# Low halves of the weights made by GpSimd instead of VectorE in the attention stages and, for every second chunk, in the opening

## The chip, the cores and the metric

The kernel runs on one core of a Trainium2 chip. The metric is the device time of one execution in microseconds, lower is better. All matrix products are done by TensorE; VectorE (DVE), ScalarE (ACT) and GpSimd (POOL) do elementwise work on data in SBUF, VectorE and ScalarE also on PSUM; SyncE (SP) issues most of the loads from device memory.

## The reference, cut to what matters

Two transformer blocks in float32 over 512 tokens of width 1024: a first block of two layers, and a second block with a recurrent branch, chunked attention, cross-attention to a memory of 256 rows, and a mixture of experts. The parts that this change touches are the products with the attention weights:

```python
for layer in range(DEPTH):                       # DEPTH = 2
    mod = sc @ w_mod[layer] + b_mod[layer]       # six vectors of 1024
    h = rmsnorm(x, g_attn[layer]) * (1.0 + scale1) + shift1
    proj = h @ w_in                              # q, k, v of three kinds of attention, 16 heads of 64 in all
    ...                                          # differential, dilated and forgetting attention
    x = x + gate1 * (o @ w_out)
    ...                                          # convolution, gated feed-forward part
# second block
...                                              # recurrent branch and chunk_band_attention: q, k, v from h @ w_in
k = (mem_n @ wk).reshape(b, m, N_XHEADS, XHEAD_DIM)   # keys and values of the memory
v = (mem_n @ wv).reshape(b, m, N_XHEADS, XHEAD_DIM)
...                                              # cross-attention, router, experts
```

## The kernel before, in words

Precision. Every float32 operand of a large product is split in two: a high half, which is the value rounded to the type that TensorE multiplies fast (`fp32r`), and a low half, the value minus the high half. A product is three matrix multiplications: high by high, high by low, low by high (`mm3`, L189). Weights are split on the chip. `wchunk` (L169) does this for one chunk of, mostly, 128 x 1024 values: SP loads it into a raw buffer `wr`, ScalarE copies it into `wh` (L176), VectorE subtracts (`wl` = `wr` - `wh`, L177). `wr`, `wh` and `wl` have three buffers each (for some chunks, asked for with `x=True`, `wh` and `wl` come from a second pool of three). So the load of a chunk can't be issued before the subtraction three chunks earlier has read its raw buffer, and `wh` and `wl` wait for TensorE's last use three chunks earlier.

Stages. The opening (`memory_kv`, L599) computes the keys and values of the memory for the much later cross-attention: 8 chunks of `xk_w` by `linear_fm`, 8 of `xv_w` by `linear_tm` (two per group of 256 columns), and, ahead of the last group, the 2 chunks of the first group of `w_qkv`. Between them it loads `x`, and computes parts of `mod` on VectorE: `mod_part` (L376) loads a 128 x 1024 piece of `w_mod` and multiplies and sums it with one instruction (L384). Results go to device memory by DMAs that GpSimd issues (`kd` L624, `vd` L636).

Then each layer of the first block runs `attention` (L829). Groups of 256 columns of `w_qkv`, two chunks each, are computed by `tm_pieces` (L474): one first group of values, ten more groups. While a group's second tile of tokens is computed, the first chunk of the next group is split (L502); after the fourth tile the second chunk, with a higher priority (L505). The matrix products are woven with the heads: scores (L396), row minimum (L399, VectorE) and exponential (L401, ScalarE), scaling (L422 or L427, VectorE), transposes (L444), a split of the transposed probabilities (L186, L187), the product with the values (L457), `operands` (L513), which turns queries and keys and splits them into `op` tiles, and `ends`, which starts the product with `w_out` (3 chunks). In layer 0 VectorE also does 27 of the `mod` parts here. GpSimd fills the unused half of an `op` tile with zeros (L554) or copies `op` tiles (L842, L843). `chunk_attention` (L1222) of the second block is built the same way: six groups, 12 chunks. The feed-forward parts, `w_out2`, the cross-attention and the experts are outside the change.

Order. Each engine works through its own queue in order. The order is planned when the program is built, by priorities and by which instructions are then expected to be ready, and `high_priority` moves instructions ahead; in the attentions the order of TensorE is the written one (`manual_schedule`).

Of the kernel before, what the change touches and what calls it, by code (L numbers as in the profile page):

```python
# [124 lines left out]
class Block:  # L125
# [43 lines left out]
    def wchunk(self, src, n, x=False):  # L169
        nc = self.nc  # L170
        raw = self.wp.tile([P, WCH], F32, tag="wr", name="wr", bufs=3)[:, :n]
        pool, nb = (self.wx, 3) if x else (self.wp, 3)
        hi = pool.tile([P, WCH], F32R, tag="wh", name="wh", bufs=nb)[:, :n]
        lo = pool.tile([P, WCH], F32R, tag="wl", name="wl", bufs=nb)[:, :n]
        nc.sync.dma_start(out=raw, in_=src)
        nc.scalar.copy(hi, raw)  # L176
        nc.vector.tensor_sub(lo, raw, hi)  # L177
        return hi, lo

    def split(self, src, hi, lo, hi_eng=None):  # L180

        nc = self.nc
        if hi_eng is nc.vector:
            nc.vector.tensor_copy(hi, src)
        else:
            nc.scalar.copy(hi, src)  # L186
        return nc.vector.tensor_sub(lo, src, hi)  # L187
# [406 lines left out]
def first_block(B, debug=None):  # L594
    with B.pool("const1") as c1:
        return first_block_(B, c1, debug)


def memory_kv(B, pool, load_x, mods, early, nxt):  # L599

    nc, I = B.nc, B.I
    kd, vd = B.kd, B.vd
    gm = pool.tile([P, KD], F32, name="gm")
    nc.sync.dma_start(out=gm, in_=I["mem_g"])
    mt = [pool.tile([P, 256], F32, name=f"m{k}") for k in range(KD)]
    nm = Norm(B, KD, D, n=256, pool=pool)
    for k in range(KD):
        nc.sync.dma_start(out=mt[k], in_=I["memT"][k])
        nm.add(k, mt[k], HALF[0])
    mn = []  # L610
    for k in range(KD):
        mn.append((pool.tile([P, 256], F32R, name=f"mh{k}"), pool.tile([P, 256], F32R, name=f"ml{k}")))
        B.gsplit(mt[k], gm[:, k:k + 1], mn[k])
    r = pool.tile([P, 2], F32, name="rm")
    nc.vector.tensor_copy(r, nm.rstd())
    R = B.spread_to(r, pool.tile([P, 256], F32, name="Rm"))

    def buf():
        return pool.tile([P, 256], F32, tag="kv", name="kv", bufs=4)

    for n in range(KD):
        t = buf()
        nc.vector.tensor_mul(t, B.linear_fm(I["xk_w"][n], mn, KD, n=256)[:, :256], R)
        nc.gpsimd.dma_start(out=kd[n], in_=t)  # L624
        load_x(XA[n])
        mods(MA[n])
    for c in range(4):
        mods(MA[8 + c])
        if c == 1:
            early()  # L630
        if c == 3:
            got = nxt()
        for j, ps in enumerate(B.linear_tm(I["xv_w"][c], mn, ntt=2)):
            t = buf()
            nc.scalar.mul(t, ps, r[:, j:j + 1])
            nc.gpsimd.dma_start(out=vd[j, :, c * 256:(c + 1) * 256], in_=t)  # L636
    return got


def first_block_(B, const, debug):  # L640
    tc, nc, I = B.tc, B.nc, B.I
# [38 lines left out]
    def load_x(n):  # L680
        for k in xs[:n]:
            nc.sync.dma_start(out=B.x[k], in_=I["xT"][k])
            nm.add(k, B.x[k], slice(0, T))
        del xs[:n]

    got = None
    if debug is None:
        got = memory_kv(B, pool, load_x, some, nm.early, lambda: B.wtm(I["w_qkv"][0, 0], x=True))
    else:
        load_x(KD)  # L690
# [11 lines left out]
    for layer in range(2):  # L702
# [31 lines left out]
        def late(n):  # L734
            B.mod_part(layer, mod, bm, todo[:n])
            del todo[:n]

        with B.pool("op") as op:
            o = [op.tile([P, T], F32, name=f"o{k}") for k in range(KD)]
            with B.pool("at") as at:  # L740
                B.at, B.nop = at, 14
                begun, oh = attention(B, layer, h, first, o, lam, sg, fb, late, I["w_out"][layer])
            if debug is not None and layer == debug[1] and debug[0] == "o":
                for k in range(KD):
                    nc.sync.dma_start(out=I["dbg"][k], in_=o[k])
                return
            B.acc_set(True)
            wb = ExitStack()
            wb.enter_context(B.extra())

            up = I["w_up"][layer]
            nm = Norm(B, KD, D)
            got = B.residual([I["w_out"][layer, n] for n in range(KD)], oh, KD, mod[:, 16:24], [nm], 2,
                             lambda: [B.wtile(up[j], KD, x=True) for j in (KF, 0, KF + 1)], begun=begun)
# [259 lines left out]
def second_block_dense(B, first, h3, debug=None):  # L1014

    tc, nc, I = B.tc, B.nc, B.I
    nm, h = mixer2(B, first)
    if debug == "m":
        return dump(B)
# [66 lines left out]
def mixer2(B, first):  # L1086


    tc, nc, I = B.tc, B.nc, B.I
# [27 lines left out]
    with B.pool("ym") as ym:  # L1117
# [76 lines left out]
                B.lnexp()  # L1194
        B.acc_set(False)
        st = {}
        with B.pool("at2") as at:
            B.at, B.nop = at, 9
            chunk_attention(B, at, h, r12, gn, ya, nr, Rr, st)
        na = st["na"]  # L1200

        def part(n, a, y, R):
            ps = B.acc()
            B.fm(ps, B.wtile(I["w_out2"][n][:, a * T:(a + 1) * T], 4), y)
            t = B.tt("yo")
            nc.vector.tensor_mul(t, ps, R)
            nc.vector.tensor_add(B.x[n], B.x[n], t)
# [705 lines left out]
```

## Time and profile before

| | |
|---|---|
| median of 3 runs | 2441.1 us (2438.98 to 2444.31) |
| the profiled execution | 2438.89 us, span 2437.1 us, mean granted TensorE clock 0.98 |
| TensorE busy | 2284.5 us (94% of the span) |
| VectorE busy | 1768.8 us (73%) |
| ScalarE busy | 1402.7 us (58%) |
| GpSimd busy | 142.9 us (6%), 136 instructions |
| L177, VectorE, all chunks | 284 instructions, 317.2 us |
| chain that ended last | TensorE 71%, VectorE 11%, L177 alone 2% |

How to read it: the span runs from the first to the last instruction of the profiled execution. Busy times of engines overlap. The chain is followed back from the last instruction, at each step to what released it, or to the instruction before it on its engine; its shares say where time was spent with nothing else late. [...] In the line groups, "x" is a count, then come the busy time in us, the mean of one in ns, the idle time of the engine just ahead of them and what ended it. A name like `wl<-wr,wh` is output and inputs.

### The profile page before, as it was taken

What the parts mean: (1) busy time and instruction counts of PE and PEld (TensorE: products, weight loads), DVE (VectorE), ACT (ScalarE), POOL (GpSimd) and SP (SyncE); (2) the same over time, 40 slices, a digit from 0 to 9 for tenths busy, and PEclk for the clock granted to TensorE, in tenths of its full rate; (3) what the DMA queues carried; (4) which work ended last, traced back from release to release, by engine and by line L of the source; (5) the groups of instructions that cost most, each with busy time, mean ns of one, the idle gap of its engine ahead of it and who ended that gap; (6) DMA issues with size and microseconds to landing.
All of it is one profiled execution on the core that took longest, in us unless ns stands there. A gap on an engine that the chain in (4) does not pass through costs nothing.

```text
span 2437.1 us, 33968 instructions
## 1 busy us (share of the span) xinstructions
PE 2284.5 (94%) x12341; PEld 1877.2 (77%) x12341; DVE 1768.8 (73%) x3246; ACT 1402.7 (58%) x2279; POOL 142.9 (6%) x136
## 2 busy tenths in 40 slices
PE   6888989999999899899999998999979999999998
PEld 6878968888888789788888887978756666666665
DVE  7899878745756897664434467687658888888888
ACT  4576764322333867643223446655427888888886
POOL 0000000000000000000000000100011111111110
PEclk9999999999999999999999999999979999999999
DMA  9623415635643111032233232214379999999992
GB/s 325 190 87 105 140 60 170 202 115 180 195 143 93 44 62 55 33 104 95 80 111 95 80 98 79 61 57 151 110 270 325 362 364 358 357 354 353 353 348 93
DMA packets 131872, 417.83 MB, mean 171 GB/s; under 512 B 22937, under 2 KB 30105, under 8 KB 131696
## 3 DMA queue, kind: packets, MB, share of 16 engines
q1 hardware_dynamic: 122832, 401.03, 48.2%
q0 software_dynamic: 8864, 14.54, 2.2%
q8 instruction: 99, 1.62, 0.3%
q14 instruction: 77, 0.63, 0.1%
HBM read 411.46 MB, written 20.19 MB: 177 GB/s over the span
## 4 chain that ended last, share of the span: by engine, by line
PE 71%; DVE 11%; issue 8%; ACT 6%; DMA 3%; SPq 0%; POOL 0%; DVEq 0%; ACTq 0%; POOLq 0%
PE acc L191 12%; PE acc L192 12%; PE acc L193 12%; PE acc L1512 8%; PE acc L1530 7%; PE acc L1513 7%; PE acc L490 2%; PE acc L491 2%; PE acc L492 2%; DVE wl L177 2%; PE s L396 1%; PE pv L457 1%; PE pt L444 1%; DVE wm L384 1%; ACT wh L176 1%
## 5 line engine op out<-in xcount | busy, mean ns | idle before, releaser
L176 ACT CAST wh<-wr 128x1024 fp32r<-128x1024 f32 (+2 forms) x284 | 272.9, 963 | 454.1 <-PE acc L192 356.0
L1480 DVE TENSOR_TENSOR ewl<-ewr,ewh 128x1024 fp32r<-128x1024 f32 x384 | 463.7, 1221 | 72.7 <-ACT ewh L1478 51.2
L177 DVE TENSOR_TENSOR wl<-wr,wh 128x1024 fp32r<-128x1024 f32 (+2 forms) x284 | 317.2, 1118 | 229.2 <-ACT wh L176 222.7
L1478 ACT CAST ewh<-ewr 128x1024 fp32r<-128x1024 f32 x384 | 397.6, 1052 | 88.5 <-PE acc L1513 54.3
L191 PE MATMUL acc<-hh,wh 128*128 128x512 f32 (+1 forms) x1088 | 411.0, 380 | 5.2 <-ACT hh L186 4.1
L192 PE MATMUL acc<-hl,wh 128*128 128x512 f32 (+1 forms) x1088 | 414.4, 381 | 0.0
L193 PE MATMUL acc<-hh,wl 128*128 128x512 f32 (+1 forms) x1088 | 411.5, 379 | 1.9 <-DVE wl L177 1.9
L191 PEld LDWEIGHTS acc<-hh,wh 128*128 128x128 f32 x1088 | 204.6, 189 | 48.3 <-ACT hh L186 4.7
L193 PEld LDWEIGHTS acc<-hh,wl 128*128 128x128 f32 x1088 | 206.1, 189 | 42.6 <-DVE wl L177 2.7
L192 PEld LDWEIGHTS acc<-hl,wh 128*128 128x128 f32 x1088 | 205.8, 189 | 40.2 <-DVE hl L187 0.2
L490 PE MATMUL acc<-wh,hh 128*128 128x256 f32 (+1 forms) x768 | 228.9, 298 | 0.0
L491 PE MATMUL acc<-wl,hh 128*128 128x256 f32 (+1 forms) x768 | 221.4, 288 | 0.0
L492 PE MATMUL acc<-wh,hl 128*128 128x256 f32 (+1 forms) x768 | 221.0, 288 | 0.0
L491 PEld LDWEIGHTS acc<-wl,hh 128*128 128x128 f32 x768 | 151.0, 197 | 2.8
L490 PEld LDWEIGHTS acc<-wh,hh 128*128 128x128 f32 x768 | 151.5, 197 | 2.0
L492 PEld LDWEIGHTS acc<-wh,hl 128*128 128x128 f32 x768 | 150.6, 196 | 0.0
L401 ACT ACTIVATE e<-e,st 128x128 f32<-128x128 f32 (+2 forms) x192 | 107.6, 561 | 69.7 <-DVE st L399 67.8
L384 DVE SCALAR_TENSOR_TENSOR wm<-wm,scb 128x1024 f32<-128x1024 f32 x96 | 116.8, 1221 | 37.3 <-DMA wm<-in_w_mod_dram 36.7
L192 PE MATMUL acc<-zl,wh 128*128 128x512 f32 (+1 forms) x363 | 141.3, 389 | 0.0
L191 PE MATMUL acc<-zh,wh 128*128 128x512 f32 (+1 forms) x363 | 141.0, 389 | 0.0
L193 PE MATMUL acc<-zh,wl 128*128 128x512 f32 (+1 forms) x363 | 140.2, 386 | 0.0
L1512 PE MATMUL acc<-ewh,xh 128*96 128x512 f32 x256 | 103.9, 406 | 12.6 <-ACT xh L186 12.6
(418 smaller groups left out, 4575.6 us busy)
## 6 DMA issues: line engine op xcount, KB each, us to landing
ewr<-in_e_gu_dram SPq DMA_DIRECT2D x256, 512.0 KB, 7.2
ewr<-in_e_dn_dram SPq DMA_DIRECT2D x128, 512.0 KB, 8.5
wm<-in_w_mod_dram SPq DMA_DIRECT2D x96, 512.0 KB, 4.2
wr<-in_w_up_dram SPq DMA_DIRECT2D x88, 512.0 KB, 3.5
wr<-in_w_qkv_dram SPq DMA_DIRECT2D x56, 512.0 KB, 3.5
wr<-in_w_down_dram SPq DMA_DIRECT2D x32, 512.0 KB, 3.6
wr<-in_w_out_dram SPq DMA_DIRECT2D x16, 512.0 KB, 3.5
wr<-in_w_down_dram SPq DMA_DIRECT2D x32, 192.0 KB, 2.3
```

The lines of the kernel that those rows point to most:

```text
L176: nc.scalar.copy(hi, raw)
L177: nc.vector.tensor_sub(lo, raw, hi)
L191: mm(ps, wh, ah, start=first, stop=False)
L192: mm(ps, wh, al, start=False, stop=False)
L193: mm(ps, wl, ah, start=False, stop=last)
L490: mm(ps, ah[:, s], wh[:, w], start=k == 0, stop=False)
L491: mm(ps, ah[:, s], wl[:, w], start=False, stop=False)
L492: mm(ps, al[:, s], wh[:, w], start=False, stop=k == KD - 1)
L1478: nc.scalar.copy(hi, raw)
L1480: nc.vector.tensor_sub(lo, raw, hi)
L1512: mm(pg, x[:, k], ww[:, :T], start=first, stop=last)
L1513: mm(pu, x[:, k], ww[:, T:], start=first, stop=last)
```

## The change

`wchunk` counts the chunks in the order in which the program is written, and gives the subtraction of L177 to GpSimd if the count modulo `pool_lo[1]` is less than `pool_lo[0]`. With (0, 1) none goes to GpSimd, with (1, 1) all, with (1, 2) every second. It is (1, 2) for the opening, (1, 1) for the two calls of `attention` and for `chunk_attention`, and (0, 1) elsewhere. Nothing else is changed: the same values are subtracted, and loads, copies, buffers and products stay.

```diff
@@ -174,8 +174,11 @@
         nc.sync.dma_start(out=raw, in_=src)
         nc.scalar.copy(hi, raw)
-        nc.vector.tensor_sub(lo, raw, hi)
+        self.nlo += 1
+        (nc.gpsimd if self.nlo % self.pool_lo[1] < self.pool_lo[0] else nc.vector).tensor_sub(lo, raw, hi)
         return hi, lo
+
+    nlo, pool_lo = 0, (0, 1)
 
@@ -684,6 +687,7 @@
     got = None
+    B.pool_lo = 1, 2
     if debug is None:
         got = memory_kv(B, pool, load_x, some, nm.early, lambda: B.wtm(I["w_qkv"][0, 0], x=True))
@@ -735,6 +739,7 @@
+        B.pool_lo = 1, 1
         with B.pool("op") as op:
@@ -745,6 +750,7 @@
             B.acc_set(True)
+            B.pool_lo = 0, 1
             wb = ExitStack()
@@ -1194,10 +1200,12 @@
+        B.pool_lo = 1, 1
         with B.pool("at2") as at:
             B.at, B.nop = at, 9
             chunk_attention(B, at, h, r12, gn, ya, nr, Rr, st)
         na = st["na"]
+        B.pool_lo = 0, 1
```

## Rows read from the trace of the kernel before

**Rows 1.** Windows: stretch; length; busy us (instructions) by engine; clock; DMA share, GB/s.

```profile
0.00:92.00 92.00, 68.03 (x510) 64.75 (x510) 72.23 (x155) 45.39 (x81) 9.15 (x20) 1.00 0.86 296
92.00:330.00 238.00, 209.74 (x1538) 198.24 (x1539) 210.29 (x623) 166.15 (x369) 17.88 (x18) 0.96 0.36 113
750.00:1002.00 252.00, 230.75 (x1741) 218.93 (x1740) 202.99 (x576) 178.78 (x392) 16.92 (x18) 0.98 0.19 61
1480.00:1600.00 120.00, 109.45 (x802) 105.35 (x801) 86.40 (x201) 73.41 (x144) 13.98 (x8) 0.94 0.21 65
```

**Rows 2.** Chain of work, shares by line, same four stretches in order.

```profile
by line: DVE wl L177 9.6%; DMA wr<-in_xk_w_dram 8.4%; DVE wm L384 7.6%; PE acc L193 7.6%; PE acc L191 7.1%; PE acc L192 6.8%; DMA wr<-in_xv_w_dram 5.2%; DMA lp<-in_lam_dram 5.2%; issue 4.8%; DMA scb<-in_c_dram 4.7%; DVE hl L341 4.5%; DVE hn
...
by line: PE acc L490 8.9%; PE acc L491 8.5%; PE acc L492 8.5%; DVE wm L384 6.2%; DMA wm<-in_w_mod_dram 5.8%; DVE wl L177 5.2%; PE s L396 4.5%; PE pv L457 3.4%; DVE e L399 3.4%; PE pt L444 3.4%; issue 3.3%; DVE op L536 2.7%; ACT e L401 2.3%;
...
by line: PE acc L490 9.0%; PE acc L492 8.7%; PE acc L491 8.6%; DVE wl L177 5.9%; PE s L396 4.4%; PE pv L457 3.7%; PE pt L444 3.4%; ACT wh L176 3.3%; ACT e L401 3.1%; ACT op L546 3.0%; issue 2.8%; DMA wr<-in_w_qkv_dram 2.8%; DVE op L536 2.6%
...
by line: issue 144.0%; PE acc L490 8.9%; PE acc L491 8.6%; PE acc L492 8.6%; PE acc L289 5.4%; PE acc L290 5.0%; PE acc L291 5.0%; DMA strip<-in_rel_dram 4.7%; DVE xc L1182 4.1%; PE s L396 4.1%; DVE wl L177 2.9%; PE pt L444 2.9%; PE pv L457
```

**Rows 3.** TensorE's waits, opening and first attention: total us, times, longest.

```profile
PE acc L290 <- DVE wl L177: 3.4, 4, 2.5
...
PE s L396 <- DVE st L399: 5.8, 4, 4.3
```

**Rows 4.** Line groups of L177, both attentions: count | busy us, mean ns | idle.

```profile
L177 DVE TENSOR_TENSOR wl<-wr,wh 128x1024 fp32r<-128x1024 f32 (+1 forms) x23 | 28.1, 1222 | 2.4 <-ACT wh L176 2.3
...
L177 DVE TENSOR_TENSOR wl<-wr,wh 128x1024 fp32r<-128x1024 f32 (+2 forms) x29 | 34.8, 1200 | 7.3 <-ACT wh L176 7.1
```

**Rows 5.** Timeline, the opening's fourth weight chunk: start us, length us, engine, line.

```profile
24.70 1.04 ACT L176 CAST wh<-wr 128x1024 fp32r<-128x1024 f32 x1
...
29.19 1.22 DVE L177 TENSOR_TENSOR wl<-wr,wh 128x1024 fp32r<-128x1024 f32 x1
...
30.44 0.33 SPq L175 DMA_DIRECT2D wr<-in_xk_w_dram  x1
```

**Rows 6.** Single lines: count, shortest/median/longest ns, first and last start us.

```profile
L554 POOL TENSOR_SCALAR op<-ones x20: 1486/1490/2510, 139.2 to 1589.9; 64x512 fp32r<-64x512 f32 x20
...
L842 POOLq EVENT_SEMAPHORE  x12: 17/2118/51387, 213.0 to 991.0; - x12
L842 POOL CAST op<-op x12: 603/608/1325, 264.5 to 993.2; 64x512 fp32r<-64x512 f32 x12
...
L1182 DVE TENSOR_TENSOR_SCAN xc<-r,i x4: 1206/1216/1625, 1483.4 to 1493.8; 128x512 f32<-128x512 f32 x4
```

**Rows 7.** Timeline, three meetings of GpSimd and VectorE instructions.

```profile
283.44 1.23 DVE L384 SCALAR_TENSOR_TENSOR wm<-wm,scb 128x1024 f32<-128x1024 f32 x1 [0.69 <-DMA wm<-in_w_mod_dram]
283.81 1.32 POOL L842 CAST op<-op 64x512 fp32r<-64x512 f32 x1 [14.13 <-issue]
...
1488.65 2.07 POOL L554 TENSOR_SCALAR op<-ones 64x512 fp32r<-64x512 f32 x1
1489.29 1.62 DVE L1182 TENSOR_TENSOR_SCAN xc<-r,i 128x512 f32<-128x512 f32 x1
...
139.24 1.51 POOL L554 TENSOR_SCALAR op<-ones 64x512 fp32r<-64x512 f32 x1 [56.01 <-PE s L396]
139.85 0.48 DVE L422 SCALAR_TENSOR_TENSOR e<-e,st 128x256 f32<-128x256 f32 x1
```

**Rows 8.** Line groups of VectorE with both sources in SBUF, both attentions: first, last.

```profile
L384 DVE SCALAR_TENSOR_TENSOR wm<-wm,scb 128x1024 f32<-128x1024 f32 x26 | 31.6, 1219 | 3.9 <-DMA wm<-in_w_mod_dram 3.9
L420 DVE TENSOR_TENSOR st<-st,lv 128x1 f32<-128x1 f32 x16 | 2.4, 150 | 0.0
...
L427 DVE TENSOR_SCALAR e<-e,st 128x128 f32<-128x128 f32 (+2 forms) x30 | 10.6, 352 | 0.7
L101 DVE TENSOR_TENSOR sqa<-sqa,sq 128x512 f32<-128x512 f32 x2 | 1.4, 683 | 0.0
```

## The prediction

> **What bounds the kernel now.** I read the table of stretches first, because the change touches four stretches only: the opening, the two attentions of the first block, and the chunk attention [rows 1]. In each the reader should compare TensorE's busy time with the length. TensorE is busy 209.7 of 238.0 us in the first attention, 230.8 of 252.0 in the second, 109.5 of 120.0 in the third, so about 28, 21 and 11 us of these are TensorE's idle time, and nothing that VectorE gives up can bring more than that. VectorE is busy 210.3 us in the first attention, as long as TensorE, and 203.0 and 86.4 in the others; GpSimd is busy for 9 to 18 us in each. The opening is another case: TensorE is busy 68.0 of 92 us, and the DMA engines run at 0.86 of their time.
>
> Then the chain of waits [rows 2]: it says how much of a stretch hangs on the subtraction of L177. That is 9.6% of 92 us = 8.8 us, 5.2% of 238 = 12.4, 5.9% of 252 = 14.9 and 2.9% of 120 = 3.5 us. Last the view of TensorE's waits: in the opening it waits for wl itself (3.4 us, four times, at L290), in the attentions never for wl but for later VectorE work that stands behind it, above all the scores' minima of L399 (5.8 us) [rows 3]. So in the attentions the subtraction costs by taking VectorE's turn, not by coming late.
>
> **What is moved.** The opening makes 18 chunks (8 of xk_w, 8 of xv_w, 2 of w_qkv), and every second goes to GpSimd: 9. Each attention of the first block makes 25 (2 for the first values, 20 for ten groups, 3 of w_out), the chunk attention 12. That is 71 of the 284 subtractions. The stretches don't end where the setting changes: two of the first attention's 25 fall into the opening's 92 us, and four of the 29 in the second attention's stretch belong to the layer before. So the stretches lose 11, 23, 25 and 12.
>
> **What VectorE gains.** One subtraction of 1024 columns takes it 1.22 us [rows 4]; 71 x 1.22 = 87 us of busy time leave it. Of that only what lies on the chain can come back: 8.8 x 11/20 = 4.9, then 12.4, 14.9 x 25/29 = 12.8, and 3.5 x 12/14 = 3.0 us, together 33 us. This is my upper end, and it is optimistic, as a chain that loses a member is followed by the next-latest one, often an activation of ScalarE.
>
> **What one costs on GpSimd.** The trace has no subtraction there. The nearest row is the copy of L842: 512 columns, one operand, 0.608 us [rows 6]. Twice the columns and two operands are four times as much to read: 4 x 0.608 = 2.4 us, and I take that. From below, if a second operand cost nothing, 1.2 us; from above, the 1.49 us of L554 for 512 columns, doubled, 3.0 us [rows 6]. At 2.4 us the stretches get 26, 55, 60 and 29 us of GpSimd work on top of 9 to 18 [rows 1], so no stretch is bound by GpSimd.
> [...]
>
> **Coming later, coming earlier.** A subtraction that takes 1.2 us longer makes wl later, unless it waited for its turn. The opening's fourth chunk shows both: its wh ends at 25.74, VectorE gets to wl at 29.19 and ends at 30.41, and the next load into that raw buffer is issued at 30.44 [rows 5]. On GpSimd wl would end near 25.74 + 2.4 = 28.1 and the load would go out 2.3 us earlier. Where VectorE is free, the loss is the 1.2 us; TensorE's four waits for wl at L290 are of that kind [rows 3], half of them are moved, so I charge 2 x 1.2 = about 2 us, and nothing for the gain on chunks like the fourth (at most the 4.9 us above). In the attentions I charge nothing: no wait of TensorE for wl is seen in the two of the first block, because a group's chunks are fetched while the group before is computed. If that cover is gone for one chunk, it costs up to 1.2 us.
>
> **What the two engines take from each other.** This is the largest unknown. The copy of L842 began 0.37 us into a 1.23 us instruction of VectorE that reads two operands from SBUF (L384), and took 1.32 us in place of 0.61: it ended 0.46 us after L384 did [rows 6, 7]. So GpSimd stands still while such an instruction runs. The other way round: the scan of L1182 met an L554 that had waited in the same manner, and took 1.625 us in place of 1.216, so VectorE lost 0.41 us [rows 6, 7]. But L422, which reads two operands too and began 0.61 us after an L554, took 0.48 us, like the others of its shape [rows 7]. I read this as: VectorE is held while GpSimd reads its operand, 0.41 us for 512 columns, and not for the rest. For two operands of 1024 columns that is 4 x 0.41 = 1.6 us of hold.
> Instructions of VectorE that read two operands from SBUF: in the first attention 141 in seven groups (26 of L384 to 16 of L420), one every 1.7 us; in the second 106 in seven groups (30 of L427 to 2 of L101), one every 2.4 us [rows 8]. Coming at random every g us, the first of them loses on average H - g(1 - exp(-H/g)) to a hold of H: 0.59 us in the first attention, 0.45 in the second. I use the first figure for the opening too, which is as crowded, and the second for the chunk attention. A loss counts as far as VectorE is on the chain; for L177 that is 12.4 of 28.1 us and 14.9 of 34.8, so 0.43 [rows 2, 4]. Sum: (11 + 23) x 0.59 x 0.43 = 8.6 and (25 + 12) x 0.45 x 0.43 = 7.2, together 16 us. The bounds are nothing (all meetings like L422's) and, with a hold of 3.0 us, 44 us.
> [...]
>
> **Queues.** The 71 subtractions join 16 DMA issues (kd, vd) and 44 fills and copies (L554, L842, L843) in GpSimd's queue, which works in order. One of these can wait long: an L842 kept the queue for up to 51 us [rows 6]. A subtraction planned behind it, and TensorE's matmul behind that, would wait as well; no such case can be seen before, so its price lies between 0 and the rival below. The kd and vd stores have buffers of their own and nobody waits for them in these stretches. On VectorE the queue gets shorter: what stood behind a subtraction that waited for its wh (2.4 and 7.3 us of idle time [rows 4]) no longer does. SP's loads and ScalarE's copies stay as they are. As each engine's order is planned when the program is built, other instructions can change places; I have no row for that.
>
> **Sum.** 33 - 16 - 2 = 15 us off. The profiled execution took 2438.9 us (span 2437.1), the median of the runs is 2441.1, 2.2 more. So 2438.9 - 15 + 2.2 = 2426 us, by its own bounds about 2415 to 2434.
>
> **Rivals.**
> First, the hold lasts as long as the GpSimd instruction, 2.4 us. The losses become 1.12 and 0.89 us: 34 x 1.12 x 0.43 + 37 x 0.89 x 0.43 = 30.5 us, and 33 - 30.5 - 2 leaves nothing: 2441 us. For: L842's standstill; against: L422. Chance 0.20.
> Second, no hold that matters, as GpSimd gives way and only it is slowed: 33 - 2 = 31 us, 2410 us. For: L422 and L842; against: L1182. Chance 0.18.
> Third, slower: the subtraction runs at L554's rate, 3.0 us, and holds VectorE throughout; then the losses are 1.60 and 1.30 us, 44 us together, 33 - 44 - 2 = 13 us lost: 2454 us. This decides from a hold of about 2.4 us upward. Place: the two attentions of the first block. For: L554 is the only arithmetic on GpSimd in the trace; against: L842 is over twice as fast. Chance 0.10.
> Fourth, GpSimd's queue: one subtraction in each of about twelve groups stands behind a fill or copy that waits for scores, and comes 2 us late for TensorE: +24 us against -15, 2450 us. For: the 51 us wait; against: the fills belong to the same unit order as the chunks, and were never waited for at length. Chance 0.07.
> The forecast keeps 0.45.
>
> **Chances.** A measurement of this kernel tells about 0.2% (5 us) from no change. Faster than that are nearly all of the forecast (0.42), the second rival (0.18) and some of the first: 0.62. The first rival and the edge of the forecast make up no change: 0.20. The third, the fourth and a part of the first are slower: 0.18. The range that leaves out two in ten runs from 2408 (just past the second rival, 2410) to 2446.
>
> **What would show it.** In the profile of the changed kernel: L177 on GpSimd 71 times, at about 2.4 us when undisturbed; VectorE's busy time in the four stretches down by 87 us less what the holds add, which would show as longer means of L384, L573 and L422; TensorE's idle time before L396, L457 and L528 down by half in the attentions; L177's share of the chain near nothing there, with no "acc <- wl" wait among TensorE's. Longer L384 and L422 by over 1 us each time would make the first rival right; waits of TensorE for wl in the attentions, the fourth. A mean over 3 us for the subtraction would make the prediction wrong.

## The result and the profile after

The changed kernel takes 2511.7 us (median of 4 runs, 2505.5 to 2518.7) against 2440.7 us of the kernel before beside it: a ratio of 1.0297, interval 1.0279 to 1.0314. It is slower by 71 us; the forecast was 2426 us, and its range ended at 2446. The profiled execution took 2513.97 us, with a span of 2512.2 us. In the kernel after, lines from L178 on stand one to eight lines lower: L177 is L178, L384 is L387, L427 is L430.

Busy time of the engines over the whole kernel, and the clock that TensorE was granted, in tenths of full speed, in 40 slices of the span:

```profile
PE 2316.3 (92%) x12341; PEld 1909.2 (76%) x12341; DVE 1771.3 (71%) x3175; ACT 1401.5 (56%) x2279; POOL 316.4 (13%) x207
PEclk9888999999999999999999999999998999999999
```

VectorE has 71 instructions fewer and is busy for longer, 1771.3 in place of 1768.8 us: the 87 us that it gave up came back in other instructions. TensorE does the same 12341 matmuls in 32 us more, and is idle for 195.9 us of the span in place of 152.6, 43 us more; together these are the 75 us between the two spans.

The stretches that answer to [rows 1], moved to where their work now lies (columns as there):

```profile
0.00:105.00 105.00, 72.81 (x467) 69.97 (x468) 75.58 (x137) 44.01 (x77) 34.52 (x30) 0.89 0.73 252
105.00:385.00 280.00, 231.12 (x1620) 217.67 (x1620) 227.99 (x633) 174.31 (x391) 79.45 (x43) 0.91 0.31 99
800.00:1065.00 265.00, 238.47 (x1751) 225.86 (x1749) 197.93 (x559) 179.73 (x399) 76.24 (x43) 0.95 0.18 58
1535.00:1660.00 125.00, 107.59 (x765) 102.08 (x765) 77.11 (x171) 74.61 (x140) 41.86 (x20) 0.93 0.22 66
```

The granted clock, here as a share of full speed, is lower in all four: 0.89, 0.91, 0.95 and 0.93 in place of 1.00, 0.96, 0.98 and 0.94, in the fourth by no more than kernels that are unchanged there differ. The windows don't hold quite the same work (TensorE makes 467, 1620, 1751 and 765 matmuls in them, where it made 510, 1538, 1741 and 802), so their busy times can't be compared one by one. Then GpSimd's subtraction itself, as a single line, and VectorE's groups in the first attention, with both sources in SBUF (first four) and with one in PSUM (last three); the columns are those of [rows 6] and [rows 8]:

```profile
L178 POOL TENSOR_TENSOR wl<-wr,wh x71: 2340/2401/3370, 15.8 to 1650.6; 128x1024 fp32r<-128x1024 f32 x67, 128x1048 fp32r<-128x1048 f32 x4
```

```profile
L387 DVE SCALAR_TENSOR_TENSOR wm<-wm,scb 128x1024 f32<-128x1024 f32 x27 | 39.2, 1451 | 9.6 <-DMA wm<-in_w_mod_dram 5.4 <-issue 2.6 <-DMA v_ln<-in_ln_dram 1.5
L576 DVE TENSOR_TENSOR qk<-qk,rp 128x256 f32<-128x256 f32 x20 | 10.7, 533 | 0.1
...
L430 DVE TENSOR_SCALAR e<-e,st 128x384 f32<-128x384 f32 x11 | 8.1, 739 | 0.2
L388 DVE TENSOR_TENSOR mod<-mod,bm 128x1 f32<-128x1 f32 x27 | 8.0, 295 | 0.2
...
L190 DVE TENSOR_TENSOR pl<-pt,ph 128x512 fp32r<-128x512 f32 x29 | 19.9, 685 | 4.4 <-ACT ph L189 4.2
L402 DVE CUSTOM_DVE_ANT_0 e<-s,c_strip 128x512 f32<-128x512 f32 x13 | 8.8, 679 | 0.2 <-PE s L399 0.2
L539 DVE SCALAR_TENSOR_TENSOR op<-pt,op 64x512 fp32r<-64x512 f32 x12 | 8.3, 689 | 0.6 <-ACT op L538 0.2
```

Before, the first four had means of 1219, 415, 410 and 154 ns; they are stretched to 1451, 533, 739 and 295. The last three had 680, 679 and 689 and stay. So it is not VectorE as a whole that is slower, but what it reads from where. Summed over all its shapes of the whole kernel (mean after less mean before, times the count), the stretching is 82 us.

In single instructions this is sharper. Taking every VectorE instruction that began while a subtraction ran on GpSimd, over 0.05 us after its begin and with at least 0.3 us of it left: the 48 that read two operands from SBUF, or are TENSOR_SCALAR on SBUF, all ended after the subtraction, even those of one column. These take 0.15 us and ended 0.01 to 0.02 us after it, so VectorE was let go about 0.14 us before GpSimd's recorded end. Of the 137 others, with an operand in PSUM or one operand only, all but two (whose own length was more than what was left) ended inside it.

TensorE's waits that answer to [rows 3], in the first attention:

```profile
PE pv L460 <- DVE pl L190: 11.5, 7, 3.1
PE pt L531 <- DVE qk L576: 10.8, 4, 3.9
PE pt L447 <- ACT e L428: 8.4, 5, 5.2
...
PE acc L494 <- POOL wl L178: 0.4, 1, 0.4
```

The first three were 5.2, 5.1 and 3.1 us before. TensorE waits there for the heads' VectorE work, hardly for GpSimd's `wl`. In the opening it does wait for `wl`, of either engine, 15.7 us in place of 6.3 (3.4 at L290 [rows 3] and 2.9 at L193). Before, then after:

```profile
PE acc L193 <- DVE wl L177: 2.9, 2, 1.5
```

```profile
PE acc L293 <- DVE wl L178: 4.8, 1, 4.8
PE acc L293 <- POOL wl L178: 4.7, 2, 2.5
PE acc L196 <- POOL wl L178: 3.3, 3, 1.9
PE acc L196 <- DVE wl L178: 2.9, 2, 2.7
```

### The profile page after: what moved, and what is told of

Read it like the earlier page. It is cut to its first block, busy times and chain, and to the rows that moved or that the text cites. A ratio compares the mean times of both kernels' runs of the same rounds, so it can differ in the third digit from the quotient of the medians.

```text
span 2512.2 us, 34001 instructions
## 1 busy us (share of the span) xinstructions
PE 2316.3 (92%) x12341; PEld 1909.2 (76%) x12341; DVE 1771.3 (71%) x3175; ACT 1401.5 (56%) x2279; POOL 316.4 (13%) x207
## 4 chain that ended last, share of the span: by engine, by line
PE 70%; issue 11%; DVE 8%; ACT 6%; DMA 3%; POOL 1%; SPq 0%; POOLq 0%; DVEq 0%; ACTq 0%
PE acc L195 11%; PE acc L194 11%; PE acc L196 11%; PE acc L1520 7%; PE acc L1538 7%; PE acc L1521 7%; PE acc L493 2%; PE acc L494 2%; PE acc L495 2%; DVE wm L387 1%; PE s L399 1%; POOL wl L178 1%; PE pv L460 1%; DMA wm<-in_w_mod_dram 1%; PE pt L447 1%
## 5 line engine op out<-in xcount | busy, mean ns | idle before, releaser
L176 ACT CAST wh<-wr 128x1024 fp32r<-128x1024 f32 (+2 forms) x284 | 272.9, 963 | 445.9 <-PE acc L195 360.6
L178 DVE TENSOR_TENSOR wl<-wr,wh 128x1024 fp32r<-128x1024 f32 (+2 forms) x213 | 230.7, 1084 | 220.0 <-ACT wh L176 213.7
L178 POOL TENSOR_TENSOR wl<-wr,wh 128x1024 fp32r<-128x1024 f32 (+1 forms) x71 | 175.8, 2484 | 1359.3 <-ACT wh L176 718.0
L195 PEld LDWEIGHTS acc<-hl,wh 128*128 128x128 f32 x1088 | 207.1, 190 | 40.4 <-DVE hl L190 0.4
L387 DVE SCALAR_TENSOR_TENSOR wm<-wm,scb 128x1024 f32<-128x1024 f32 x96 | 126.2, 1314 | 45.5 <-DMA wm<-in_w_mod_dram 41.2
```

The source lines that it names most:

```text
L178: (nc.gpsimd if self.nlo % self.pool_lo[1] < self.pool_lo[0] else nc.vector).tensor_sub(lo, raw, hi)
L195: mm(ps, wh, al, start=False, stop=False)
```

## The experiments

To see where time goes I use the starts of ScalarE's copies of L176, counted from 0 as the chunks come: chunks 0 to 17 are the opening's, 18 to 42 the first attention's, 126 to 150 the second's, 240 to 251 the chunk attention's. (The expectations that speak of "the tenth" and "the eighteenth chunk" mean numbers 10 and 18.) The table has the us between such starts in the profiled execution of each kernel. Its second row is the spread over kernels whose work is the same there: differences of up to 5 us mean nothing. It leaves out one value: e13_open_twice took 281.8 us in chunks 18-43, where its edit changes nothing, so a difference of 7 us can arise there by other ways than the one under test.

| kernel | chunks 0-10 | 10-18 | 18-43 | 124-151 | 240-252 |
|---|---|---|---|---|---|
| before | 40.4 | 27.3 | 274.6 | 277.7 | 98.8 |
| kernels unchanged there | 39.3-42.0 | 26.4-28.2 | 272.9-277.1 | 273.4-278.0 | 96.5-101.8 |
| after | 52.5 | 36.2 | 301.1 | 289.6 | 105.2 |
| e1_open | 52.8 | 36.1 | 273.2 | 273.5 | 99.0 |
| e2_att | 40.4 | 27.9 | 304.3 | 288.6 | 96.5 |
| e3_chunk | 39.3 | 27.8 | 272.9 | 277.6 | 109.2 |
| e4_add_sub | 40.7 | 27.4 | 321.0 | 302.3 | 101.4 |
| e6_no_sub | 42.0 | 28.2 | 270.3 | 270.3 | 98.7 |
| e7_sub_unread | 40.3 | 28.0 | 298.3 | 290.1 | 101.8 |
| e5_add_copies | 41.4 | 27.0 | 299.3 | 283.0 | 96.9 |
| e12_att_quarters | 40.8 | 26.4 | 292.0 | 277.2 | 101.6 |
| e11_before_one_store | 40.7 | 26.5 | 274.5 | 277.5 | 101.7 |
| e10_open_one_store | 49.2 | 34.8 | 276.5 | 277.9 | 98.9 |
| e13_open_twice | 41.9 | 30.2 | 281.8 | 273.4 | 99.8 |
| e14_open_unread | 50.2 | 27.8 | 277.1 | 278.0 | 98.9 |

**One stage alone.** The theory after the result was exclusion: VectorE stands still for the whole of a GpSimd subtraction. The rivals were lateness of `wl`, GpSimd's queue, a relief worth less than the chain said, and another planned order of the instructions. First the change in one stage at a time; for e1_open:

```diff
-        B.pool_lo = 1, 1
+        B.pool_lo = 0, 1
         with B.pool("op") as op:
...
-        B.pool_lo = 1, 1
+        B.pool_lo = 0, 1
         with B.pool("at2") as at:
```

e2_att and e3_chunk leave the setting on in their stage only.

> The change in the opening alone: 9 of its 18 subtractions on GpSimd, none elsewhere. In the trace of the changed kernel the first attention starts some 18 to 20 us later than before. If that loss is the opening's own, this kernel takes 2459 us (before 2441) and everything behind the opening is as before. If the loss is a matter of the plan of the whole program, it takes about 2441 us.

> The change in the two attentions of the first block alone: 50 subtractions on GpSimd. In the trace of the changed kernel these stretches lose 27 and 12 us. If the stretches' losses add up: 2441 + 39 = 2480 us. If the first attention only suffers from what the opening leaves it: about 2460 us.

> The change in the chunk attention alone, 12 subtractions. The changed kernel lost 10 us in this stretch; if the parts add up, this gives 2446 to 2455 us. By exclusion at the rate of the first block's second attention (25 subtractions, 10 to 13 us) it would be about 5 us, 2441 to 2449 us; by the forecast's own sum (a gain of 3.0 less a loss of 2.3 us) no change, 2440 us.

Measured: e1_open 2461.8 us, ratio 1.0096 (1.0059 to 1.0134); e2_att 2481.8 us, 1.0162 (1.0130 to 1.0195); e3_chunk 2447.6 us, 1.0030 (1.0016 to 1.0045). The parts are +22, +42 and +8.5 us; their sum, 73 us, stands beside the 71 us of the whole. Every stage loses. (The time of e3_chunk lies in two of its three expected ranges, so it doesn't tell whether the chunk attention loses by exclusion at the rate of the second attention or more; its stretch lost 10.4 us.)

**The reading without the relief, and the relief without the reading.** In the 50 chunks of the two attentions, e4_add_sub leaves the subtraction on VectorE and adds an idle one on GpSimd:

```diff
         nc.vector.tensor_sub(lo, raw, hi)
+        if self.nlo % self.pool_lo[1] < self.pool_lo[0]:
+            nc.gpsimd.tensor_sub(raw, raw, hi)
```

and e6_no_sub makes none, neither here nor there:

```diff
+        if self.nlo % self.pool_lo[1] < self.pool_lo[0]:
+            return hi, hi
         nc.vector.tensor_sub(lo, raw, hi)
```

> VectorE keeps all its subtractions; beside that GpSimd does a subtraction of the same size for each of the 50 chunks of the two attentions, written into the raw buffer once VectorE has read it, and nobody reads the result. No weight comes later and VectorE gets no relief. Theory one (the two engines exclude each other, and VectorE loses about 1.2 us for each): VectorE's instructions with two operands in SBUF get longer by some 50 us in all, and the kernel takes 2470 to 2500 us. Theory two (the loss of the change is that weights come later): 2441 us, within 5.

> No subtraction at all for the 50 chunks of the two attentions; the products take the high half in place of the low half (the low halves are left out of the result). This is VectorE's relief alone. By the chain of waits before, 12.4 + 12.8 = 25 us: 2416 us. If the freed time is filled by other late work (a chain's next member), half of it: 2429 us. If the relief was worth nothing in the first place: 2441 us.

Measured: e4_add_sub 2516.9 us, ratio 1.0317 (1.0277 to 1.0357). GpSimd's reading alone costs 46.4 + 24.6 = 71 us in the two attentions, though nobody needs what it makes (part of it may be that it keeps the raw buffer longer). The whole time lies above the 2470 to 2500 us of theory one; theory two is out.

The same run answers the rival of the order. When the subtractions leave VectorE, the planner moves its other work too: in the trace of e2_att only about 460 of the 661 other VectorE instructions of chunks 18 to 42, and about 540 of the 592 of chunks 126 to 150, stand in the sequence of the kernel before. In e4_add_sub about 640 of the 661 and all 592 do, and it loses 71 us: exclusion costs that much with the order hardly touched. What the other order alone costs was not measured. VectorE's shortest two-operand instruction shows what happens in e4_add_sub; before, it took 151 ns:

```profile
L425 DVE TENSOR_TENSOR st<-st,lv 128x1 f32<-128x1 f32 x32 | 16.6, 520 | 0.1
```

e6_no_sub shows what the relief is worth with no reading in its way: 270.3 us in both attentions, 4.3 and 7.4 less than before, and 2.6 to 6.8 and 3.1 to 7.7 less than the kernels unchanged there. That is 6 to 15 us, the changed order included, where the chain's shares had promised 25. Its time as a whole, 3297 us, says nothing: with other values the experts get other rows, and TensorE makes 13501 matmuls in place of 12341.

**The reading without the lateness.** e7_sub_unread makes GpSimd's subtraction and does not use it:

```diff
+        if self.nlo % self.pool_lo[1] < self.pool_lo[0]:
+            nc.gpsimd.tensor_sub(lo, raw, hi)
+            return hi, hi
         nc.vector.tensor_sub(lo, raw, hi)
```

> The two attentions of the first block as in the change, with GpSimd's subtraction made for all 50 chunks, but its result is not read: TensorE multiplies with wh where it took wl. That changes the values, the router then sends other rows to the experts, and only the time up to the experts is comparable. Nobody waits for the subtraction now, except the next load into its raw buffer and the next subtraction into its output. If the loss of the attentions is lateness (TensorE waiting for a wl that comes 1.2 us later), it goes: 0 to -9 us against the kernel before, as with no subtraction at all. If it is the exclusion, it stays: +24 to +30 us by the end of the first attention, +33 to +43 by the end of the second, and VectorE's instructions are stretched by 50 to 60 us.

The loss stays: 298.3 and 290.1 us, 28.0 and 19.8 more than e6_no_sub, which differs from it in the program by GpSimd's instruction alone (its whole time, 3348 us, says as little). VectorE's order is the same in both in the second attention; in the first it differs, so the 28.0 us may hold some of that. With it, the exclusion costs 47.8 us, for 56.7 us of stretched VectorE instructions: 0.84 us of time for each (0.89 in the second attention alone). This weight is no constant, as the copies below show. Against e2_att (304.3 and 288.6) lateness is worth 6.0 and -1.5 us, 4.5 together, within the spread.

**How long an instruction excludes.** Two copies in place of the added subtraction (e5_add_copies), and the subtraction in four quarters of its columns (e12_att_quarters):

```diff
         nc.vector.tensor_sub(lo, raw, hi)
+        if self.nlo % self.pool_lo[1] < self.pool_lo[0]:
+            for _ in range(2):
+                nc.gpsimd.tensor_copy(raw, hi)
```

```diff
+            for q in range(4):
+                s = slice(q * n // 4, (q + 1) * n // 4)
+                nc.gpsimd.tensor_sub(lo[:, s], raw[:, s], hi[:, s])
```

> VectorE keeps all its subtractions, and in the two attentions of the first block GpSimd makes, for each of the 50 chunks, two copies of wh into the raw buffer, which nobody reads (one operand from SBUF each, where the added subtraction had two). Each copy should take about 1.2 us undisturbed, so GpSimd reads for as long as with the added subtraction. If any GpSimd instruction that reads SBUF excludes VectorE for its whole length, this costs the same as the added subtraction did: about +47 us by the end of the first attention, +71 by the end of the second, 2500 to 2520 us, and VectorE's instructions are stretched by about 55 us. If only the second operand's path is shared, it costs under 10 us: 2440 to 2450, and VectorE's durations stay.

> The two attentions of the first block as in the change, each subtraction of GpSimd cut into four of a quarter of the columns, about 0.62 us each. If an instruction excludes for its whole length and no longer, the mean loss of a VectorE instruction that meets one falls with the square of the length: by H - g(1 - exp(-H/g)) with H 0.62 and g 1.7 and 2.4 us, 0.10 and 0.07 us for each quarter, so 25 x 0.40 + 25 x 0.29 = 17 us stretched in place of 56. With the relief of 9 us and some lateness that makes about 2440 to 2455 us. If both engines share the path evenly over time, the stretching depends on what GpSimd reads, not on the pieces: about 55 us again and 2475 to 2485 us. If it is lateness alone, about 2475 to 2485 us too, but without stretched instructions.

GpSimd's instruction of e5_add_copies, and that of e12_att_quarters (shortest, median, longest ns):

```profile
L181 POOL COPY wr<-wh x100: 1035/1047/3749, 88.6 to 1031.8; 128x1024 f32<-128x1024 f32 x92, 128x1048 f32<-128x1048 f32 x8
```

```profile
L181 POOL TENSOR_TENSOR wl<-wr,wh x200: 713/738/1751, 81.8 to 1017.7; 128x256 fp32r<-128x256 f32 x92, 128x262 fp32r<-128x262 f32 x8
```

e5_add_copies took 2475.8 us, 1.0150 (1.0131 to 1.0169), and e12_att_quarters 2457.2 us, 1.0077 (1.0051 to 1.0102). Neither rival of e5 held: it costs something between the two. In its first attention 24.7 us are lost for 15.4 us of stretched instructions, in its second 5.3 us for 9.6. The size follows from the length of one instruction. The forecast's formula for the mean loss, H - g(1 - exp(-H/g)) with g of 1.7 and 2.4 us, gives with H of 1.047 us 0.27 and 0.20 us, over 50 copies in each attention 23 us; stretched were 24.0 us. With H of 0.738 it gives 0.14 and 0.10, over 100 quarters each 24 us; stretched were 24.2. With H of 2.40 and 25 each it gives 50; stretched were 55.6 in e2_att and 55.0 in e4_add_sub. (These sums leave out VectorE's own subtractions, which the g doesn't count: another 7.8 us in e4_add_sub and 1.1 in e5_add_copies.) The 17 us and 2440 to 2455 us expected of e12_att_quarters were a little low, as a quarter had been put at 0.62 us; rivals two and three, 2475 us or more, are out. So one operand suffices, and a copy or a subtraction excludes for its own length and no longer: cutting it into four, though it read as much and ran longer in all (2.95 in place of 2.40 us), more than halved the harm, with VectorE's order in both attentions the same as in e2_att. It does not make a gain: the second attention is back at 277.2 us, the first still loses 17.

**The opening: GpSimd's queue.** In e1_open the subtractions begin up to 8.2 us after their `wh`, because kd stores that wait for VectorE's product stand ahead of them. The first try put the stores behind all chunks in the program, with 16 buffers; e9 is the kernel before with the same stores:

```diff
-        nc.gpsimd.dma_start(out=kd[n], in_=t)
+        late.append((kd[n], t))
...
+    for d, t in late:
+        nc.gpsimd.dma_start(out=d, in_=t)
```

> The opening as in the change (every second subtraction on GpSimd), and GpSimd's 16 stores of kd and vd put behind all chunks of the opening, with a buffer for each, so that no subtraction can stand behind a store that waits for VectorE. To be read against the kernel before with its stores moved in the same way. If GpSimd's queue makes the opening's loss (subtractions up to 9.7 us late), most of the 15 to 22 us that the opening's part alone cost comes back: 2 to 8 us slower than its control, with each subtraction starting within 1 us of its wh. If the exclusion of the two engines makes it, the loss stays at 13 to 20 us, and VectorE's instructions with two SBUF operands are as long as with the stores in their place (18 us added in all).

> Control: the kernel before with the 16 stores of kd and vd moved behind all chunks of the opening, a buffer for each. Nobody reads kd and vd until the second block, so every theory expects the time of the kernel before, 2440 us within 5.

Measured 2461.7 us, 1.0092 (1.0075 to 1.0109), and 2438.7 us, 1.0000 (0.9990 to 1.0010). But the planner had put the stores back where they were, as GpSimd's timeline of e8 shows, so this decides nothing:

```profile
34.65 0.55 POOL L643 DMA_DIRECT2D kd<-kv  x1 [2.52 <-DVE kv L628]
40.68 0.54 POOL L643 DMA_DIRECT2D kd<-kv  x1 [5.48 <-DVE kv L628]
41.24 2.48 POOL L178 TENSOR_TENSOR wl<-wr,wh 128x1024 fp32r<-128x1024 f32 x1
```

This subtraction's `wh` had ended at 32.5 us. The second try leaves one store, which can't run before the last product:

```diff
+    kt = pool.tile([P, 4 * D], F32, name="kt")
...
-        nc.gpsimd.dma_start(out=kd[n], in_=t)
...
+    nc.gpsimd.dma_start(out=B.kvd, in_=kt)
```

> The opening as in the change, but kd and vd are collected in one tile and stored by one DMA behind the last product, so that GpSimd's queue holds the nine subtractions and then that one store; no subtraction can stand behind a store that waits for VectorE. If the head of GpSimd's queue makes the opening's loss, it falls from 17 to 20 us at the eighteenth chunk to 3 to 8 us, TensorE waits less than 6 us for wl in place of 15, and the time is within 2440 to 2448 us. If the exclusion makes it, 13 us or more stay, with 16 to 18 us of stretched VectorE instructions, and the time is 2455 us or more.

> Control: the kernel before with the same single store of kd and vd behind the last product of the opening. In the kernel before GpSimd has nothing but these stores there, and nobody reads them until the second block: every theory expects 2440 us within 5, and the landmarks of the opening within 2 us.

Measured 2457.8 us, 1.0073 (1.0049 to 1.0096), and 2439.9 us, 1.0005 (0.9991 to 1.0020). With the queue clear, the opening still loses 18 us; the queue was worth about 4, and as the intervals of e1 and e10 overlap, even these are not sure. The queue falls as the main cause. GpSimd and VectorE in e10 (start, length; only these two engines' lines) show the exclusion in both directions:

```profile
24.38 1.22 DVE L178 TENSOR_TENSOR wl<-wr,wh 128x1024 fp32r<-128x1024 f32 x1
24.92 2.92 POOL L178 TENSOR_TENSOR wl<-wr,wh 128x1024 fp32r<-128x1024 f32 x1 [5.99 <-ACT wh L176]
25.51 2.89 DVE L101 TENSOR_TENSOR sqa<-sqa,sq 128x512 f32<-128x512 f32 x1
```

VectorE's subtraction came first and ended at 25.60; GpSimd's, begun at 24.92, took 2.92 us in place of 2.40. L101, normally 0.68 us, then waited for GpSimd until shortly before its end at 27.84 and took 2.89.

**The opening: exclusion or lateness.** With the same single store, VectorE makes every second subtraction twice (lateness without exclusion), or GpSimd makes it and TensorE doesn't use it (exclusion without lateness):

```diff
         nc.vector.tensor_sub(lo, raw, hi)
+        if self.nlo % self.pool_lo[1] < self.pool_lo[0]:
+            nc.vector.tensor_sub(lo, raw, hi)
```

```diff
+        if self.nlo % self.pool_lo[1] < self.pool_lo[0]:
+            nc.gpsimd.tensor_sub(lo, raw, hi)
+            return hi, hi
```

> The opening with the single late store and no GpSimd subtraction: VectorE makes every second subtraction twice, so that wl of these nine chunks comes 1.22 us later without another engine's reading. With GpSimd and the same store the eighteenth chunk came 16.6 us later than in the control, 8.2 of it between the tenth and the eighteenth, where the subtraction starts right after its wh. If that second half is lateness, this kernel loses 4 to 6 us there (four chunks of 1.22 us, where GpSimd's took 1.2 to 2.1 us longer); if it is the exclusion, it loses under 2 us there. The whole time: 2445 to 2452 us by the first, about 2442 to 2446 us by the second.

> The opening with the single late store and GpSimd's nine subtractions made, but TensorE multiplies with wh where it took the wl of GpSimd; that changes values and so the experts' work, and only the landmarks up to the experts are comparable. The exclusion is there, the lateness is not. If lateness makes the loss between the tenth and the eighteenth chunk (8.2 us), it is under 2 us here; if the exclusion makes the loss of the first ten chunks (8.4 us), 5 to 8 us of that stay. If neither falls, the exclusion makes both halves.

Against the control e11, e10 loses 8.5 us in chunks 0-10 and 8.3 in 10-18. e14, with exclusion and no lateness, loses 9.5 and 1.3 (its whole time, 2453.9 us, is no measure, as its values differ); e13, with lateness and no exclusion, 1.2 and 3.7 (its time is 2452.2 us, 1.0049 with 1.0030 to 1.0069; it loses another 7 us in the first attention, for a reason that stays open). So the first half is lost by exclusion: VectorE is crowded with `mod_part` and norms there.

Most of the second half goes when nobody waits for GpSimd's `wl`: it is lost by lateness. There VectorE's subtraction had begun 0.03 to 0.39 us after its `wh`, so moving it saved hardly a turn, and in e10 each of four `wl` ended 0.9 to 2.2 us later after its `wh` than in e11. TensorE's waits for `wl` in chunks 10-18, in e11, then in e10:

```profile
PE acc L290 <- DVE wl L177: 1.5, 4, 0.6
```

```profile
PE acc L293 <- POOL wl L178: 5.3, 2, 2.7
```

The rest of the 8.3 us is partly TensorE's clock: 27.5 us busy at a granted clock of 0.90 in place of 24.8 at 1.00, for nearly the same matmuls (199 and 194). Two of GpSimd's four subtractions are themselves stretched, to 3.12 and 3.36 us, by a VectorE instruction that had begun before them. Two limits: e14 has no control that leaves out the subtraction, as e6 is for e7, and it also spares waits that e11 has (1.5 us in the second half), so exclusion may cost up to about 3 us there. And e13 is not lateness alone: the repeated subtractions take turns of a crowded VectorE, and in two of the four chunks `wl` ends 3.54 us after `wh`, later than e10's 3.20 and 3.44. Why it still loses only 3.7 us is not shown.

## Why the prediction was wrong

**What is moved, and the length: right.** 71 subtractions at a median of 2401 ns; the 2.4 us were taken as four times the copy of [rows 6].

**The hold: wrong.** It took 4 x 0.41 = 1.6 us per subtraction from one meeting of L1182 [rows 7], and let L422's undisturbed run beside an L554 speak against a longer one. The runs show the full 2.4 us less the last 0.14, for every two-operand instruction in SBUF that met a subtraction, and e5 and e12 show that it goes with the length of the instruction. The forecast's 16 us stand for 37 us of stretched instructions at its weight of 0.43; 82 us were stretched. That is the first rival's mechanism, and its prices of 1.12 and 0.89 us per subtraction (50 us for the 50) stand close to the 55.6 us stretched. In the count above 48 of 48 were held that read two operands from SBUF or are TENSOR_SCALAR on SBUF, while `pl`, which reads one operand from PSUM, took 685 ns where it had taken 680.

L422's run was real, but L554 was the wrong instruction to scale from: a fill held VectorE only in its first 0.40 to 0.47 us. The trace of the kernel before shows both kinds. A fill, and L1181 (0.69 us by its median) beginning 0.32 us into it; then a copy of L843, and L385 (0.15 us) beginning 0.29 us into it:

```profile
1487.08 1.49 POOL L554 TENSOR_SCALAR op<-ones 64x512 fp32r<-64x512 f32 x1 [491.92 <-ACT l L1177]
1487.40 0.84 DVE L1181 TENSOR_TENSOR i<-i,l 128x512 f32<-128x512 f32 x1
...
269.07 0.61 POOL L843 CAST op<-ones 2x512 fp32r<-2x512 f32 x1
269.36 0.33 DVE L385 TENSOR_TENSOR mod<-mod,bm 128x1 f32<-128x1 f32 x1
```

L1181 lost 0.15 us and L385 0.18, so each was let go about 0.47 us after GpSimd began: with 1.02 us of the fill still to run, but only 0.14 us of the copy. L422 began at 0.61 us. Over the traces of all kernels, 35 VectorE instructions with two SBUF operands, or TENSOR_SCALAR on SBUF, began in the first 0.46 us of an undisturbed fill, and all were let go 0.40 to 0.47 us after its begin; 75 began later, up to 0.2 us before its end, and none lost more than 0.04 us. So the fill let VectorE go early, where the subtraction held it until 0.14 us before its end; why is not shown. The copy, with its 0.47 of 0.61 us, was the row to price a subtraction by.

**The weight of a loss: wrong, about as costly as the hold.** The forecast counted 0.43 us of time for each us lost, L177's share of its own time on the chain. e7 against e6 gives 0.84, with the spread by stage named above. The instructions that were held are not L177: they are those at the end of a head, `qk` and what stands ahead of `pl`, for which TensorE waits (11.5 and 10.8 us in the rows above), and with the longer waits the granted clock was lower (0.91 in place of 0.96 in the first attention). In e2_att TensorE is busy for 2303.1 us, 18.6 more than before, out of 42 lost. With 0.84 in place of 0.43, by the prediction's own sum, the first rival would have lost 60 us in place of 30.5, and 33 - 60 - 2 would have made it 29 us slower, not even.

**The relief: wrong by a factor of two to four in the attentions.** The chain's 12.4 + 12.8 = 25 us were called optimistic; without any subtraction there, 6 to 15 us came back (e6). Here a share of the chain was not what was gained when its member went. That the next-latest work stands right behind it, as the prediction itself warned, is the likely reason; e6 doesn't show it.

**Lateness and queues: wrong in the opening, right in the attentions.** The 2 us charged for four waits at L290 became 8.3 us in chunks 10-18 (e10), of which 1.3 stay without lateness (e14). The step looked at TensorE's waits, and of these left out the two at L193 (2.9 us); it should have looked at how soon VectorE began after `wh`, for a subtraction that begins at once gains nothing by moving and loses the difference in length. That the kd stores cost nothing, as nobody waits for them, was wrong in kind: subtractions stood behind them, up to 8.2 us. The price is small, about 4 us. In the attentions, where nothing was charged, it is 4.5 us within a spread as large.

**The sum with the measured terms.** In the stretches of the two attentions: relief 4.3 + 7.4 = 11.7 back, exclusion 47.8 and lateness 4.5 lost, which makes the 40.6 us that e2_att lost there (the three differences add up to it by their making; its whole time rose by 42). In the opening, chunks 0 to 18: 10.8 with exclusion and no lateness, 4.9 with lateness and no exclusion, 16.8 with both, and 21.2 with the queue (e1_open, whose whole time rose by 22). The chunk attention adds 8.5, by its whole time. Together 40.6 + 21.2 + 8.5 = 70 us, beside the 71 measured, where the forecast had 15 us off.

**The chances.** Slower had 0.18, and its own mechanism (third rival, a hold of 3.0 us) gave 2454. The right hold stood at 0.20, with a price that the weight of 0.43 had halved. The two errors had one source: the price of the hold was taken from few meetings, and the weight of a lost microsecond from an instruction that was not the one to lose it.

## What to carry to other kernels

GpSimd's elementwise work beside a busy VectorE was not free engine time here: every VectorE instruction with two operands in SBUF that met a subtraction waited for its end, less 0.14 us (48 of 48 in the count above, TENSOR_SCALAR on SBUF among them), and a subtraction of 1.22 us moved off VectorE cost it 1.1 us of standing still and, at 0.84, nearly as much time (0.84 on the mean of two stages; 0.55 and 1.6 in the two stages of e5). Before such a move, count VectorE's two-operand SBUF instructions in the stretch and price the loss by H - g(1 - exp(-H/g)) with the whole length H of a copy or a subtraction (the fill of L554 held for 0.47 of its 1.49 us); if it must be done, four short instructions harmed less than one long one (24.2 us stretched in e12_att_quarters, 55.6 in e2_att), and VectorE's work with an operand in PSUM was not harmed (`pl`: 685 ns, before 680). And a step that starts the moment its input is there has no turn to give back: moved to a slower engine, it comes later by its whole extra length (here each of four `wl` by 0.9 to 2.2 us, e10 against e11), and where something waits for it that is lost.

## What the runs showed of the hardware that was not expected

A VectorE instruction of one column, 0.16 us, took 2.17 us beside a GpSimd subtraction (timeline of the kernel after, VectorE, then GpSimd):

```profile
57.14 2.17 DVE L388 TENSOR_TENSOR mod<-mod,bm 128x1 f32<-128x1 f32 x1
```

```profile
56.81 2.48 POOL L178 TENSOR_TENSOR wl<-wr,wh 128x1024 fp32r<-128x1024 f32 x1
```

TENSOR_SCALAR with one tensor in SBUF (L430: 410 to 739 ns) was held like two-operand instructions, while a RECIPROCAL in SBUF was not (159 ns, before 158): 12 of 12 `e<-e,st` and none of 29 in the count above.
